# Hybrid decoder layer: gate and up's products and transposes pinned to program order on TensorE, two small norm loads moved

## The chip, the cores and the metric

The kernel runs on one core of a Trainium2 chip. A core has five engines with queues of their own: TensorE (PE, matmuls and transposes), VectorE (DVE), ScalarE (ACT), GpSimd (POOL) and SyncE (SP, which issues most DMAs here). The metric is the device time of one execution in microseconds (us); lower is better.

## The reference

A decoder layer on 1024 rows of width 1024, all in float32:

```
x = x + 0.5 * SwiGLU_1(RMSNorm(x))          # w_gate, w_up: 1024 x 2816, w_down: 2816 x 1024
h = RMSNorm(x); p = h @ W_in
o_A = dilated window attention(p)            # 8 heads of 64; q and k are normed per head
o_B = latent attention(p)                    # 4 heads
x = x + W_out [RMSNorm(o_A); RMSNorm(o_B)]
x = x + 0.5 * SwiGLU_2(RMSNorm(x))

SwiGLU(h) = (silu(h @ w_gate) * (h @ w_up)) @ w_down
```

The change touches the two SwiGLU blocks (FFN1 and FFN2 below) and the loads of the two norm weights `dil_q_norm` and `dil_k_norm` of o_A's heads.

## The kernel before, in words

**Products.** Each float32 operand is split into a high part (an ACT copy, L104) and a low part (a DVE subtraction, L105). `products()` then issues, for each of four blocks of 128 rows, three matmuls: high by high (L125), high by low (L126), low by high (L127). One product of the FFN is thus 12 matmuls of 128x512, all into one PSUM bank. There are eight banks (`ps()`).

**Gate and up by Strassen's scheme.** The 2816 columns are cut into 11 pairs c = 0 to 10. For each pair and each of gate ("g") and up ("u"), in short a unit such as 0g, seven products replace eight: M11, M12, S1, S3, S2, S4, M22. The activations' operands (B11, B21, B22, T1 to T4) are made once from the transposed, normed rows. The weights' operands (S1 to S4 are sums and differences of weight blocks, L326) are made ahead by `prepare()`; AHEAD is 5 products. For c < FRONT = 4, M11 and M12 run first, for all pairs, while the later rows still arrive, and their sum goes to DRAM (`p1`). So a unit with c < 4 later runs only:

```
middle:  S1 -> Dk,  S3 -> E,  S2 -> A;   a = kept + A (L583);  q = a + E (L584);  q = q + Dk (L585)
close:   S4 -> Dk (accumulates);  q = a + Dk (L593);  M22 -> E (accumulates);  a = a + E (L597)
```

`kept` is M11+M12 read back from `p1`. The program's order for these pairs is middle(0g), close(0g), middle(0u), close(0u), middle(1g), and so on. From c = 4 on, M11 and M12 of the next unit are written between a middle and its close; for 3u they are those of 4g.

**What sets the order.** A scheduler builds every engine's order from the program and from a modelled timeline; a bare instruction may be moved past its neighbours if its data allow it. `tc.keep_in_program_order(i)` ties an instruction to the one of the same engine that was traced before it, as an order of issue. `behind_operands()` places DVE's sums behind the low parts of the next operands (LEAD = 3).

**Start of an FFN.** `bank(th, k)` makes one bank of transposed rows: four 128x128 transposes (L232), one from each row tile. Tiles `y[0]` to `y[3]` are half 0 of the rows and `y[4]` to `y[7]` half 1, which `second_half()` turns between the early products. Row norms go ACT (squares), POOL (L193, L135, L136: the reciprocal root), DVE (scaling).

**Norm weights.** `qkgain`, two columns of 128, is loaded by two POOL DMAs (L81) at the start of the kernel, and its first column is scaled by DVE (L82). It is used in the attention part, far behind FFN1. `rel_bias_rows()` prepares the attention's bias rows; it is called beside FFN1, in pieces.

Of the kernel before, what the change touches and what calls it, by code (L numbers as in the profile page):

```python
# [13 lines left out]
ALU = mybir.AluOpType  # L14
# [4 lines left out]
P = 128  # L19
# [11 lines left out]
HD = 64  # L31
# [30 lines left out]
def tile_layer(ctx: ExitStack, tc: tile.TileContext, x, g1n, mixn, g2n, wg1, wu1, wd1, wg2, wu2, wd2,  # L62
               w_in, dqn, dkn, rel_t, qan, wqb, kvan, wkvb, mqn, mkn, ond, onm, w_out,
               cs, onehot, mask, out):
    nc = tc.nc
# [8 lines left out]
    ident = cpool.tile([P, P], F32, name="ident")  # L74
# [2 lines left out]
    nc.gpsimd.memset(neghalf, -0.5)  # L77
    qkgain = cpool.tile([P, 2], F32, name="qkgain")
    kpss = cpool.tile([P, NT], F32, name="kpss")
    for i, src in enumerate((dqn, dkn)):  # L80
        nc.gpsimd.dma_start(qkgain[:, i:i + 1], bass.AP(src.tensor, src.offset, [[0, 2], [1, HD], [1, 1]]))  # L81
    nc.vector.tensor_scalar(qkgain[:, 0:1], qkgain[:, 0:1], -HD ** -0.5, None, op0=ALU.mult)  # L82

    count = [0]

    def nm(s):
        count[0] += 1
        return f"{s}_{count[0]}"

    def slot(shape, dt=F32):  # L90
        return slots.tile(shape, dt, tag="slot", name=nm("slot"))

    def tmp(shape, dt=F32):
        return tpool.tile(shape, dt, tag="tmp", name=nm("tmp"))

    def small(w):
        return spool.tile([P, 8], F32, tag="small", name=nm("small"))[:, :w]

    def ps():
        return psum.tile([P, 512], F32, tag="ps", name=nm("ps"))  # L100
# [16 lines left out]
        split(hi[:, :cols], lo[:, :cols], raw[:, :cols])  # L117
        return hi, lo

    def products(pt, pairs, first=True):  # L120


        total = len(pairs)
        for i, ((ah, al), (bh, bl)) in enumerate(pairs):
            nc.tensor.matmul(pt, ah, bh, start=first and i == 0, stop=False, skip_group_check=not first)  # L125
            nc.tensor.matmul(pt, ah, bl, start=False, stop=False, skip_group_check=not first)  # L126
            nc.tensor.matmul(pt, al, bh, start=False, stop=i == total - 1, skip_group_check=not first)  # L127

    def cut(pair, a, b):
        return pair[0][:, a:b], pair[1][:, a:b]  # L130
# [92 lines left out]
    def ffn(rows_in, ys, gain, wg, wu, wd, act_d, xsrc, done, lead, aside=iter(())):  # L223
# [2 lines left out]

        y = {}

        def bank(th, k):
            pt = ps()  # L230
            for i in range(4):
                nc.tensor.transpose(pt[:, i * P:(i + 1) * P], y[4 * th + i][:, k * P:(k + 1) * P], ident)  # L232
            return pt

        B11, B21, B22, T1, T2, T3, T4 = (Block() for _ in range(7))
        w21, b12 = [], []

        def column(kf):
            return gcol[:, kf:kf + 1]

        def plain(of, k, pt, kf):

            if k % 2 == 0:
                of.append(slot([P, 2, 512]))
            nc.scalar.activation(of[-1][:, k % 2, :], pt, AF.Copy, scale=column(kf))

        def half(of, k):
            return of[k // 2][:, k % 2, :]

        def second_half():  # L250


            for k in range(4):
                plain(b12, k, bank(1, k), k)
            yield
            banks = [bank(1, 4 + k) for k in range(4)]
            yield
            t1 = []
            for k in range(4):
                hi, lo = B11.hi_lo(k)  # L260
                t1.append(tmp([P, 512]))
                nc.vector.tensor_tensor(t1[k], hi.bitcast(F32), lo.bitcast(F32), op=ALU.add)
                nc.vector.tensor_tensor(t1[k], half(b12, k), t1[k], op=ALU.subtract)
                T1.put(k, t1[k])
                B22.put(k, banks[k], column(4 + k))
                t = half(b12, k)
                nc.vector.scalar_tensor_tensor(t, banks[k], column(4 + k), t, op0=ALU.mult, op1=ALU.subtract)
                nc.vector.scalar_tensor_tensor(t1[k], banks[k], column(4 + k), t1[k], op0=ALU.mult, op1=ALU.subtract)
                yield
            for k in range(4):  # L270
                T3.put(k, half(b12, k))
            yield
            for k in range(4):
                T2.put(k, t1[k])
            yield
            for k in range(4):
                t = half(w21, k)
                nc.vector.tensor_tensor(t, t, t1[k], op=ALU.subtract)
                T4.put(k, t)
            yield  # L280
# [30 lines left out]
        def make(c, nme, which):  # L311
            front = c < FRONT and which in ("M11", "M12")
            u = (front, c, nme)
            load_units(units.index(u) + (3 if front else 2))
            f1, f2 = raws[u][0], raws[u][-1]
            m = {"M11": f1[:, :512], "M12": f1[:, 512:], "M21": f2[:, :512], "M22": f2[:, 512:]}
            need = {"S1": ("M21", "M22", ALU.add), "S2": ("S1", "M11", ALU.subtract),
                    "S3": ("M11", "M21", ALU.subtract), "S4": ("M12", "S2", ALU.subtract)}
            if which in need:

                a_, b_, op = need[which]
                if which == "S1":
                    sums_["S1"] = tmp([P, 512])
                s1 = sums_["S1"]
                src = {"S1": s1, "S3": m["M21"], "S2": s1, "S4": m["M12"]}[which]
                nc.vector.tensor_tensor(src, s1 if a_ == "S1" else m[a_], s1 if b_ == "S2" else m[b_], op=op)  # L326
            else:
                src = m[which]
            s = slot([P, 2, 512], F32R)
            lows.append(split(s[:, 0, :], s[:, 1, :], src))  # L330
            ready[(c, nme, which)] = (s[:, 0, :], s[:, 1, :])
            if which == "M22" or (front and which == "M12"):
                del raws[u]
# [8 lines left out]
        def prepare(n):  # L342
            while made[0] < min(used[0] + n, len(order)):
                make(*order[made[0]])
                made[0] += 1

        def product(pt, c, nme, which, blk, first=True, ahead=AHEAD):
            assert order[used[0]] == (c, nme, which)
            prepare(ahead + 1)
            used[0] += 1  # L350
            w = ready.pop((c, nme, which))
            products(pt, [(cut(w, k * P, (k + 1) * P), blk.hi_lo(k)) for k in range(4)], first)

        acts = {}

# [67 lines left out]
        for t in range(4 + lead):  # L423
            y[t] = ys(t)
        prepare(1)
        for k in range(4):
            B11.put(k, bank(0, k), column(k))
        prepare(2)
        banks = [bank(0, 4 + k) for k in range(4)]
        for k in range(4):  # L430
            B21.put(k, banks[k], column(4 + k))
        sums = second_half()

        def hook(n):
# [123 lines left out]
        def start(c, nme):  # L558

            A, Bk = ps(), ps()  # L560
            product(A, c, nme, "M11", B11)
            product(Bk, c, nme, "M12", B21)
            q = tmp([P, 512])
            nc.scalar.activation(q, A, AF.Copy)
            with behind_operands():
                nc.vector.tensor_tensor(q, q, Bk, op=ALU.add)  # L566
            return A, q
# [81 lines left out]
    def rel_bias_rows():  # L649
        oh = [slot([P, RW // 2]) for _ in range(2)]  # L650
        br = [slot([P, RW // 2]) for _ in range(2)]
        rt = small(8)
        nc.gpsimd.memset(rt[:33, :], 1.0)
        nc.sync.dma_start(rt[:32, :], rel_t)
        w = RW // 2
        for c in range(2):
            nc.sync.dma_start(oh[c][:33, :], onehot[:, c * w:(c + 1) * w])
        yield
        for c in range(2):
            for j in range(2):  # L660
                pt = ps()
                sl = slice(j * w // 2, (j + 1) * w // 2)
                nc.tensor.matmul(pt[:8, :w // 2], rt[:33, :8], oh[c][:33, sl], start=True, stop=True)
                nc.vector.tensor_copy(br[c][:8, sl], pt[:8, :w // 2])
            nc.gpsimd.dma_start(brd[:, c * w:(c + 1) * w], br[c][:8, :])
        for i in range(2):
            nc.gpsimd.dma_start(bd[:, :, i, :], bass.AP(brd.tensor, brd.offset + i * NEAR + 127,
                                                        [[RW, DH], [-1, P], [1, 256]]))
        yield

    def columns(src, col, width):
# [17 lines left out]
    def mid(t, xt):  # L689
# [11 lines left out]
        defer(2 if t < 4 else 4, turn)  # L701

    ffn(load_rows, lambda t: norm_rows(x0.pop(t), both=t < 4), g1n, wg1, wu1, wd1, act_d, x, mid, 0, rel_bias_rows())


# [643 lines left out]
    def fin(t, xt):  # L1349
        nc.sync.dma_start(out[t * P:(t + 1) * P, :], xt)  # L1350

    ffn(lambda t: None, last_rows, g2n, wg2, wu2, wd2, act_d, x2, fin, 2)
    flush()

# [75 lines left out]
```

## Time and profile before

| | us |
|---|---|
| runs: median (3) | 1892.15 |
| runs: lowest, highest | 1885.06, 1893.9 |
| profiled execution, own time | 1884.57 |
| its span | 1882.8 |
| PE busy in the span | 1821.7 (97%) |
| DVE, ACT, POOL busy | 1241.4, 789.9, 295.3 |
| FFN1, gate and up and down | 0 to about 640 |
| attention | about 640 to 1200 |
| FFN2 | about 1200 to 1880 |

The span is what the profile of one execution covers; that execution's own time is 1.8 us more. In the profile's rows an engine is busy while it executes; matmuls overlap, one of 128x512 lasts 0.39 us, but the next starts after about 0.23. Matmul rows are of a modelled end, and a few can be missing.

### The profile page before, as it was taken

The numbers are of one execution on the slowest core, as the hardware profiler recorded it, in microseconds if no ns is written. First come the engines' busy times: TensorE is split into PE (matmuls) and PEld (weight loads), VectorE is DVE, ScalarE is ACT, GpSimd is POOL, SyncE is SP. The second block draws the span as 40 slices with busy tenths as digits, with TensorE's granted clock in tenths as the row PEclk, the third lists the DMA queues.
The fourth block names the chain that finished last, engine by engine and source line by source line (L and its number), as shares of the span: only waits on it lengthen the run. The fifth ranks groups of instructions, "written<-read, shape, count | busy, mean of one in ns | idle before, by whom it ended". The sixth has DMA issues, their size and how long they took to land.

```text
span 1882.8 us, 25065 instructions
## 1 busy us (share of the span) xinstructions
PE 1821.7 (97%) x9040; PEld 1534.8 (82%) x9040; DVE 1241.4 (66%) x2375; ACT 789.9 (42%) x1802; POOL 295.3 (16%) x508
## 2 busy tenths in 40 slices
PE   7998999999999999999998999998999999999998
PEld 6776888888888888889997988886778888888887
DVE  5867767666968273327878783467776766778671
ACT  6422332334445152235876682363223333343540
POOL 3011010000000122423455520210111000100000
PEclk9999999999999999999999999999999999999999
DMA  7334233325943241023311232333433322388412
GB/s 252 123 120 145 107 133 116 116 74 201 383 148 112 95 139 34 29 57 113 96 31 36 69 118 101 117 146 106 156 101 134 107 86 94 115 306 294 124 56 90
DMA packets 92325, 234.38 MB, mean 124 GB/s; under 512 B 12486, under 2 KB 18328, under 8 KB 92200
## 3 DMA queue, kind: packets, MB, share of 16 engines
q1 hardware_dynamic: 71592, 162.93, 26.1%
q0 software_dynamic: 20608, 69.85, 10.6%
q8 instruction: 71, 1.16, 0.3%
q14 instruction: 54, 0.44, 0.1%
HBM read 165.00 MB, written 63.53 MB: 121 GB/s over the span
## 4 chain that ended last, share of the span: by engine, by line
PE 86%; DVE 8%; ACT 2%; issue 2%; DMA 1%; SPq 0%; POOL 0%; DVEq 0%; POOLq 0%; ACTq 0%
PE ps L127 19%; PE ps L125 18%; PE ps L126 18%; PE ps L516 7%; PE ps L517 7%; PE ps L515 7%; DVE slot L105 2%; PE ps L839 2%; PE ps L865 1%; PE ps L813 1%; PE ps L904 1%; PE ps L829 1%; DMA slot<-in_wg_dram 1%; ACT slot L104 1%; PE ps L1027 1%
## 5 line engine op out<-in xcount | busy, mean ns | idle before, releaser
L125 PE MATMUL ps<-slot,slot 128*128 128x512 f32 (+3 forms) x1712 | 659.1, 387 | 11.9 <-ACT slot L104 9.6
L127 PE MATMUL ps<-slot,slot 128*128 128x512 f32 (+3 forms) x1712 | 652.4, 385 | 13.8 <-DVE slot L105 13.8
L126 PE MATMUL ps<-slot,slot 128*128 128x512 f32 (+3 forms) x1712 | 655.7, 383 | 3.6 <-DVE slot L105 3.6
L127 PEld LDWEIGHTS ps<-slot,slot 128*128 128x128 f32 x1712 | 323.2, 189 | 81.2 <-DVE slot L105 19.5
L125 PEld LDWEIGHTS ps<-slot,slot 128*128 128x128 f32 x1712 | 323.0, 189 | 80.4 <-ACT slot L104 16.7
L126 PEld LDWEIGHTS ps<-slot,slot 128*128 128x128 f32 x1712 | 323.2, 189 | 65.5 <-DVE slot L105 4.4
L105 DVE TENSOR_TENSOR slot<-slot,slot 128x512 fp32r<-128x512 f32 (+1 forms) x428 | 293.2, 704 | 42.9 <-ACT slot L104 41.2
L104 ACT ACTIVATE slot<-slot 128x512 fp32r<-128x512 f32 (+1 forms) x428 | 261.0, 638 | 110.3 <-PE ps L517 49.0
L104 ACT ACTIVATE slot<-tmp 128x512 fp32r<-128x512 f32 x258 | 160.5, 626 | 311.3 <-DVE tmp L326 212.7
L516 PE MATMUL ps<-slot,slot 128*128 128x512 f32 x616 | 239.9, 390 | 0.0
L517 PE MATMUL ps<-slot,slot 128*128 128x512 f32 x616 | 239.7, 389 | 0.0
L515 PE MATMUL ps<-slot,slot 128*128 128x512 f32 x616 | 237.0, 389 | 0.0
L105 DVE TENSOR_TENSOR slot<-tmp,slot 128x512 fp32r<-128x512 f32 x258 | 176.4, 687 | 21.6 <-ACT slot L104 21.0
L515 PEld LDWEIGHTS ps<-slot,slot 128*128 128x128 f32 x616 | 115.6, 188 | 24.0
L516 PEld LDWEIGHTS ps<-slot,slot 128*128 128x128 f32 x616 | 115.6, 188 | 24.0
L517 PEld LDWEIGHTS ps<-slot,slot 128*128 128x128 f32 x616 | 115.6, 188 | 23.9
L593 DVE TENSOR_TENSOR tmp<-tmp,ps 128x512 f32<-128x512 f32 x44 | 30.3, 688 | 135.2 <-PE ps L127 135.2
L601 ACT ACTIVATE tmp<-tmp 128x512 f32<-128x512 f32 x80 | 50.3, 629 | 157.7 <-DVE tmp L593 118.1
L523 DVE SCALAR_TENSOR_TENSOR slot<-ps,slot 128x512 f32<-128x512 f32 x56 | 37.4, 688 | 81.4 <-PE ps L517 81.4
L821 ACT ACTIVATE slot<-slot,tmp 128x256 f32<-128x256 f32 (+1 forms) x128 | 59.7, 468 | 27.6 <-DVE tmp L814 26.9
L136 POOL TENSOR_TENSOR small<-small,neghalf 128x1 f32<-128x1 f32 (+2 forms) x68 | 66.6, 982 | 5.0
L566 DVE TENSOR_TENSOR tmp<-tmp,ps 128x512 f32<-128x512 f32 x28 | 19.3, 688 | 72.6 <-PE ps L127 72.6
(180 smaller groups left out, 1995.3 us busy)
## 6 DMA issues: line engine op xcount, KB each, us to landing
tmp<-act SPq DMA_DIRECT2D x154, 256.0 KB
act<-slot POOLq DMA_DIRECT2D x58, 512.0 KB, 5.0
slot<-in_wg_dram SPq DMA_DIRECT2D x52, 512.0 KB
slot<-in_wu_dram SPq DMA_DIRECT2D x52, 512.0 KB
slot<-in_wd_dram SPq DMA_DIRECT2D x40, 512.0 KB
slot<-in_x_dram SPq DMA_DIRECT2D x16, 512.0 KB
x_mid<-slot POOLq DMA_DIRECT2D x16, 512.0 KB, 3.7
slot<-x_mid SPq DMA_DIRECT2D x16, 512.0 KB
```

The costliest lines, as they stand in the source:

```text
L104: nc.scalar.activation(hi, src, AF.Copy)
L105: return nc.vector.tensor_tensor(lo, src, hi.bitcast(F32), op=ALU.subtract)
L125: nc.tensor.matmul(pt, ah, bh, start=first and i == 0, stop=False, skip_group_check=not first)
L126: nc.tensor.matmul(pt, ah, bl, start=False, stop=False, skip_group_check=not first)
L127: nc.tensor.matmul(pt, al, bh, start=False, stop=i == total - 1, skip_group_check=not first)
L136: nc.gpsimd.tensor_tensor(r, r, neghalf[:, :w], op=ALU.pow)
L515: nc.tensor.matmul(banks[i], ah, w[:, 0, :], start=first and k == 0, stop=False, skip_group_check=not first)
L516: nc.tensor.matmul(banks[i], ah, w[:, 1, :], start=False, stop=False, skip_group_check=not first)
L517: nc.tensor.matmul(banks[i], al, w[:, 0, :], start=False, stop=k == KD - 1, skip_group_check=not first)
L601: nc.scalar.activation(q, q, AF.Silu)
L821: nc.scalar.activation(self.p[:, e, :w], self.p[:, e, :w], AF.Exp, bias=self.m[e], scale=-1.0, accum_out=self.den[e])
L839: nc.tensor.matmul(po[:, e * HD:(e + 1) * HD], self.pt[:, n * P:(n + 1) * P], self.head["values"](self.far, self.j, e, j - nb + 1), start= ...
```

## The change

Three edits.

1. All matmuls of gate's and up's products are pinned by `tc.keep_in_program_order` (argument `pin` of `products()`, given by `product()`). Other users of `products()` are not pinned.
2. `bank()` becomes `turned()`: several banks are transposed together, one row tile after the other through all banks, and the transposes are pinned. Half 0's eight banks are made together before the first operands are.
3. The two loads of `qkgain` and DVE's scaling of it move into `rel_bias_rows()`, pinned.

In the changed file L125, L126, L127 are L122, L124, L126; L105 is L102; L326 is L328; L583, L584, L585 are L586, L587, L588; L593 and L597 are L596 and L600.

```
-    for i, src in enumerate((dqn, dkn)):
-        nc.gpsimd.dma_start(qkgain[:, i:i + 1], bass.AP(src.tensor, src.offset, [[0, 2], [1, HD], [1, 1]]))
-    nc.vector.tensor_scalar(qkgain[:, 0:1], qkgain[:, 0:1], -HD ** -0.5, None, op0=ALU.mult)
...
-    def products(pt, pairs, first=True):
+    def products(pt, pairs, first=True, pin=lambda i: i):
...
-            nc.tensor.matmul(pt, ah, bh, start=first and i == 0, stop=False, skip_group_check=not first)
...
+            pin(nc.tensor.matmul(pt, ah, bh, start=first and i == 0, stop=False,
+                                 skip_group_check=not first))
...
-        def bank(th, k):
-            pt = ps()
+        def turned(th, ks):
+            pts = [ps() for _ in ks]
             for i in range(4):
-                nc.tensor.transpose(pt[:, i * P:(i + 1) * P], y[4 * th + i][:, k * P:(k + 1) * P], ident)
-            return pt
+                for pt, k in zip(pts, ks):
+                    tc.keep_in_program_order(
+                        nc.tensor.transpose(pt[:, i * P:(i + 1) * P], y[4 * th + i][:, k * P:(k + 1) * P], ident))
+            return pts
...
-            for k in range(4):
-                plain(b12, k, bank(1, k), k)
+            for k, pt in enumerate(turned(1, range(4))):
+                plain(b12, k, pt, k)
             yield
-            banks = [bank(1, 4 + k) for k in range(4)]
+            banks = turned(1, range(4, 8))
...
-            products(pt, [(cut(w, k * P, (k + 1) * P), blk.hi_lo(k)) for k in range(4)], first)
+            products(pt, [(cut(w, k * P, (k + 1) * P), blk.hi_lo(k)) for k in range(4)], first,
+                     tc.keep_in_program_order)
...
+        banks = turned(0, range(8))
         for k in range(4):
-            B11.put(k, bank(0, k), column(k))
+            B11.put(k, banks.pop(0), column(k))
         prepare(2)
-        banks = [bank(0, 4 + k) for k in range(4)]
...   (in rel_bias_rows)
+        for i, src in enumerate((dqn, dkn)):
+            tc.keep_in_program_order(
+                nc.gpsimd.dma_start(qkgain[:, i:i + 1], bass.AP(src.tensor, src.offset, [[0, 2], [1, HD], [1, 1]])))
...
+        tc.keep_in_program_order(
+            nc.vector.tensor_scalar(qkgain[:, 0:1], qkgain[:, 0:1], -HD ** -0.5, None, op0=ALU.mult))
```

How the order moves, at three places. On PE, the end of S2 of unit 0g in FFN1, before (ps_155 is its bank A, ps_148 its Dk, ps_149 its E; ps_163 and ps_164 are Dk and E of the next unit, 0u; slots are operands):

```order
L125 MATMUL ps_155_762<-slot_138_665,slot_135_656 128x512
L125 MATMUL ps_163_823<-slot_109_513,slot_153_731 128x512
L126 MATMUL ps_163_823<-slot_110_514,slot_153_731 128x512
L126 MATMUL ps_155_762<-slot_139_666,slot_135_656 128x512
L127 MATMUL ps_155_762<-slot_138_665,slot_135_656 128x512
L125 MATMUL ps_164_824<-slot_129_626,slot_154_747 128x512
L126 MATMUL ps_164_824<-slot_130_627,slot_154_747 128x512
L127 MATMUL ps_163_823<-slot_109_513,slot_153_731 128x512
```

The rest of S1 and S3 of 0u, M22 of 0g and two matmuls of S2 of 0u follow; S4 of 0g (into ps_148) begins 36 matmuls behind the last of S2. And now:

```order
L122 MATMUL ps_155_759<-slot_138_662,slot_135_653 128x512
L124 MATMUL ps_155_759<-slot_139_663,slot_135_653 128x512
L126 MATMUL ps_155_759<-slot_138_662,slot_135_653 128x512
L122 MATMUL ps_148_720<-slot_111_514,slot_140_681 128x512
L124 MATMUL ps_148_720<-slot_112_515,slot_140_681 128x512
```

S4 of 0g stands directly behind S2's last matmul; M22 of 0g follows, then S1, S3, S2 of 0u, each whole.

On DVE, the sums behind S2 of unit 1g, before (ps_189 is A, ps_183 E, ps_182 Dk):

```order
L583 TENSOR_TENSOR tmp_192_994<-tmp_190_976,ps_189_975 128x512
L105 TENSOR_TENSOR slot_188_960<-slot_166_827,slot_188_960 128x512
L383 TENSOR_TENSOR slot_180_928<-slot_180_928,slot_175_886 128x512
L326 TENSOR_TENSOR tmp_186_942<-tmp_186_942,slot_165_825 128x512
L584 TENSOR_TENSOR tmp_193_995<-tmp_192_994,ps_183_937 128x512
L385 TENSOR_TENSOR slot_181_929<-slot_178_908,slot_180_928 128x512
L326 TENSOR_TENSOR slot_165_825<-slot_165_825,tmp_186_942 128x512
L585 TENSOR_TENSOR tmp_193_995<-tmp_193_995,ps_182_936 128x512
```

And now:

```order
L586 TENSOR_TENSOR tmp_192_991<-tmp_190_973,ps_189_972 128x512
L102 TENSOR_TENSOR slot_196_1016<-slot_166_824,slot_196_1016 128x512
L587 TENSOR_TENSOR tmp_193_992<-tmp_192_991,ps_183_934 128x512
L588 TENSOR_TENSOR tmp_193_992<-tmp_193_992,ps_182_933 128x512
L596 TENSOR_TENSOR tmp_195_1013<-tmp_192_991,ps_182_933 128x512
```

One low part is left between the three sums, where five operations stood before; L596, the sum behind S4, is next.

On POOL, the end of row 7's norm in FFN1, before:

```order
L193 TENSOR_TENSOR small_69_294<-small_67_290 128x1
L135 TENSOR_SCALAR small_70_296<-small_69_294 128x1
L653 MEMSET small_282_1531 33x8
L136 TENSOR_TENSOR small_70_296<-small_70_296,neghalf_77 128x1
L401 DMA p1_88<-slot_76_328 128x1024
```

And now:

```order
L193 TENSOR_TENSOR small_69_291<-small_67_287 128x1
L135 TENSOR_SCALAR small_70_293<-small_69_291 128x1
L656 MEMSET small_282_1528 33x8
L663 DMA qkgain_79<-in_dqn_dram 128x1x1
L663 DMA qkgain_79<-in_dkn_dram 128x1x1
L136 TENSOR_TENSOR small_70_293<-small_70_293,neghalf_77 128x1
L404 DMA p1_85<-slot_76_325 128x1024
```

The two loads of the norm weights stand between two steps of the last row's norm.

More of the change, by code (lines that the diff above doesn't have):

```diff
@@ L118, in load_unit @@
         return hi, lo
-    def products(pt, pairs, first=True):
+    def products(pt, pairs, first=True, pin=lambda i: i):
         total = len(pairs)
         for i, ((ah, al), (bh, bl)) in enumerate(pairs):
-            nc.tensor.matmul(pt, ah, bh, start=first and i == 0, stop=False, skip_group_check=not first)
-            nc.tensor.matmul(pt, ah, bl, start=False, stop=False, skip_group_check=not first)
-            nc.tensor.matmul(pt, al, bh, start=False, stop=i == total - 1, skip_group_check=not first)
+            pin(nc.tensor.matmul(pt, ah, bh, start=first and i == 0, stop=False,
+                                 skip_group_check=not first))
+            pin(nc.tensor.matmul(pt, ah, bl, start=False, stop=False,
+                                 skip_group_check=not first))
+            pin(nc.tensor.matmul(pt, al, bh, start=False, stop=i == total - 1,
+                                 skip_group_check=not first))
     def cut(pair, a, b):
```

## The prediction

> **What bounds the kernel now.** I read the page first (engine shares, the chain that ended last, the costliest groups), then the waits of TensorE (PE), then windows of time, then single instructions where the windows show loss.
>
> ```profile
> span 1882.8 us, 25065 instructions
> PE 1821.7 (97%) x9040; PEld 1534.8 (82%) x9040; DVE 1241.4 (66%) x2375; ACT 789.9 (42%) x1802; POOL 295.3 (16%) x508
> PE 86%; DVE 8%; ACT 2%; issue 2%; DMA 1%; SPq 0%; POOL 0%; DVEq 0%; POOLq 0%; ACTq 0%
> ...
> PE ps L127 <- DVE slot L105: 13.8, 13, 1.6
> PE ps L232 <- DVE slot L198: 11.9, 2, 11.5
> PE ps L125 <- ACT slot L104: 9.6, 13, 1.1
> ...
> PE ps L126 <- DVE slot L105: 3.6, 2, 1.8
> ```
>
> PE is the bound: busy 97% of the span and 86% of the chain. The waits (us in total, times, longest) say where it idles. The 11.9 us at L232 are the kernel's start, for the input rows. The other three lines, 27.0 us in 28 waits, are matmuls of gate and up that wait for the high part (ACT, L104) or the low part (DVE, L105) of an operand. Only these can be won back.
>
> ```profile
> 60.00:95.40 35.40, 31.02 (x127) 24.36 (x125) 28.40 (x48) 12.43 (x23) 2.71 (x5) 0.95 0.37 126
> 95.40:190.00 94.60, 84.91 (x352) 66.12 (x352) 64.24 (x106) 23.57 (x40) 12.54 (x21) 0.98 0.40 136
> 200.00:300.00 100.00, 100.00 (x443) 82.00 (x442) 67.59 (x112) 32.57 (x56) 10.82 (x15) 1.00 0.37 127
> 1275.00:1300.00 25.00, 20.55 (x82) 15.90 (x81) 19.83 (x34) 10.87 (x20) 2.46 (x5) 0.93 0.39 132
> 1300.00:1400.00 100.00, 91.56 (x385) 72.10 (x384) 69.91 (x115) 25.60 (x44) 12.52 (x21) 0.98 0.40 136
> ...
> 1400.00:1500.00 100.00, 100.00 (x443) 82.81 (x442) 67.69 (x110) 34.53 (x61) 7.97 (x12) 1.00 0.29 106
> ```
>
> Each row: window, its length, then busy time and count for PE, weight loads, DVE, ACT, POOL, then granted clock. In 200 to 300 and 1400 to 1500 PE never rests: 443 matmuls in 100 us, 0.2257 us each. By that rate the four other windows lose 35.4-127x0.2257 = 6.7, 94.6-352x0.2257 = 15.2, 25-82x0.2257 = 6.5 and 100-385x0.2257 = 13.1 us, 41.5 us together. All of it lies where the pairs c=0 to 3 run S1, S3, S2, S4, M22 (their M11 and M12 were done earlier), once in each FFN. That is all the change can win.
>
> **What pinning does there.** S4 accumulates into bank Dk, which S1 filled, and DVE must first read Dk for the sum over S2 (L583 reads S2's bank, L584 adds E, L585 adds Dk). So S4 waits for L585. Before, the scheduler put other products between.
>
> ```profile
> 77.30 0.39 PE L127 MATMUL ps<-slot,slot 128*128 128x512 f32 x1
> 78.68 0.50 PE L125 MATMUL ps<-slot,slot 128*128 128x512 f32 x1 [1.00 <-ACT slot L104]
> ...
> 81.03 0.50 PE L127 MATMUL ps<-slot,slot 128*128 128x512 f32 x1 [1.61 <-DVE slot L105]
> 81.37 0.39 PE L125 MATMUL ps<-slot,slot 128*128 128x512 f32 x1
> ...
> 90.46 0.39 PE L125 MATMUL ps<-slot,slot 128*128 128x512 f32 x1
> ...
> 92.95 0.62 PE L127 MATMUL ps<-slot,slot 128*128 128x512 f32 x2
> ...
> 95.45 0.50 PE L125 MATMUL ps<-slot,slot 128*128 128x512 f32 x1
> ...
> 1301.49 0.39 PE L125 MATMUL ps<-slot,slot 128*128 128x512 f32 x1
> ...
> 80.29 0.69 DVE L105 TENSOR_TENSOR slot<-tmp,slot 128x512 fp32r<-128x512 f32 x1
> ...
> 83.89 0.68 DVE L585 TENSOR_TENSOR tmp<-tmp,ps 128x512 f32<-128x512 f32 x1
> ...
> 93.38 0.69 DVE L593 TENSOR_TENSOR tmp<-tmp,ps 128x512 f32<-128x512 f32 x1 [7.00 <-PE ps L127]
> ...
> 193.80 0.68 DVE L584 TENSOR_TENSOR tmp<-tmp,ps 128x512 f32<-128x512 f32 x1
> 194.52 0.69 DVE L585 TENSOR_TENSOR tmp<-tmp,ps 128x512 f32<-128x512 f32 x1
> ...
> 1290.02 0.69 DVE L585 TENSOR_TENSOR tmp<-tmp,ps 128x512 f32<-128x512 f32 x1
> ```
>
> For the first gate unit S2's last matmul starts at 77.30; L585 ends at 83.89+0.68 = 84.57; S4 starts at 90.46, with 36 matmuls of the next unit and M22 in between. Afterwards S4's first matmul stands right behind S2's last.
>
> Short windows around the two first units, columns as above:
>
> ```profile
> 71.78:75.19 3.41, 1.64 (x7) 1.04 (x6) 3.41 (x7) 3.41 (x7) 1.07 (x2) 1.00 0.99 382
> ...
> 78.61:82.02 3.41, 1.72 (x6) 1.15 (x7) 3.41 (x6) 0.02 (x1) 0.54 (x1) 1.00 0.19 54
> 82.02:85.43 3.41, 3.41 (x9) 2.64 (x9) 3.41 (x7) 2.00 (x4) 0.00 (x0) 0.50 0.06 23
> ...
> 1283.52:1286.93 3.41, 0.98 (x4) 0.30 (x2) 3.41 (x6) 0.63 (x1) 0.54 (x1) 1.00 0.11 25
> 1286.93:1290.34 3.41, 3.18 (x8) 2.50 (x9) 3.41 (x7) 0.78 (x2) 0.00 (x0) 0.50 0.14 52
> ```
>
> *First unit of each FFN.* DVE fills these windows (3.41 of 3.41) and is the bound there, so L585 ends no earlier than 84.57. S4 then starts 0.05 later (the L105 at 80.29 ended at 80.98, and the matmul that waited for it started at 81.03), its first matmul takes 0.34 in place of 0.227 (81.03 to 81.37), and five products follow up to the point that before reaches at 95.45: 84.62+0.11+60x0.2267 = 98.33, so +2.9. In FFN2 the same from 1290.71: 1304.47 against 1301.49, +3.0.
>
> *The other closes with no cover.* 0u, 1g, 1u, 2g, 2u and 3g: six in each FFN. From the last matmul's start to DVE's first read 0.43 (92.95 to 93.38); L583 to L584 and L584 to L585 0.72 each, the spacing of dependent ones (193.80 to 194.52); L585 0.69; 0.05 to the matmul; 0.11 for its slow start; less 0.227 for the normal step: 2.49. In gate units from 1g on the new DVE order has one L105 between L583 and L584, about 0.5 more: 2.97. Three of each: 16.4 us for each FFN. In return these stretches' own losses go, since S4 and M22 give ACT and DVE five products of lead: 15.2 and 13.1. Net +1.2 and +3.3. The ends: 2.1 a close if the DVE steps are 0.60 apart as independent ones are, 3.6 if two more operations slip in.
>
> *Covered closes.* For 3u and all c from 4 on, M11 and M12 of the next unit stand between S2 and S4, in both kernels.
>
> ```profile
> 230.15 0.39 PE L125 MATMUL ps<-slot,slot 128*128 128x512 f32 x1
> ...
> 231.70 0.69 DVE L585 TENSOR_TENSOR tmp<-tmp,ps 128x512 f32<-128x512 f32 x1
> ...
> 235.59 0.39 PE L125 MATMUL ps<-slot,slot 128*128 128x512 f32 x1
> ```
>
> S2 ends near 230.15, L585 at 232.39, M12 near 235.59: 3.2 us to spare, so nothing. If that cover were gone, 2.5 us for each of 30 closes.
>
> **The small parts.** The norm weights' loads and their DVE scaling leave the start; PE's start waits for input rows, so 0 (at most 0.5). On POOL the two loads now stand ahead of the last step of row 7's norm (L136):
>
> ```profile
> 1.31 1.03 POOL L81 DMA_DIRECT2D qkgain<-in_dqn_dram  x1 [0.35 <-issue]
> 2.34 0.82 POOL L81 DMA_DIRECT2D qkgain<-in_dkn_dram  x1
> ...
> 32.23 0.63 POOL L136 TENSOR_TENSOR small<-small,neghalf 128x1 f32<-128x1 f32 x1
> ```
>
> That step and the four transposes that need it come 1.85 later. The queued matmuls cover some of it; between 0 and 1.85 I take 0.9, the middle, because pinned transposes hold the banks that DVE reads next. Transposing several banks row by row in FFN2 delays its first operand by up to 2 us, of which earlier products cover more than half: 0.7, between 0 and 2.
>
> Sum so far: 0.9+2.9+1.2+0.7+3.0+3.3 = +12.0.
>
> **The clock.** Bubbles have a second price, in the short windows above. The granted clock is 0.50 for 3.41 us after a window with 6 matmuls or fewer (78.61, 1283.52), and was not lowered after one with 7 (71.78). Two of the four such windows in these stages are shown, all on one grid of 3.41 us; the sums above already credit the old ones. A half-clock window issues 9 where 15 would go: 1.4 to 1.7 us, say 1.5. A window has 6 matmuls or fewer if at least 3.41-6.5x0.2267 = 1.94 us of a bubble falls in it. For a bubble of 2.49 that fails when the grid cuts it so that neither part reaches 1.94, 1.39/3.41 = 41% of positions; for 2.97, 27%. So 66% of twelve closes dip: 12x0.66x1.5 = 11.9, and the two long first bubbles for certain: 3.0.
>
> The Trainium skill ("TensorE: Matmul & The Clock Gate", Part 1 and "HAM oscillation") puts the free-running window at 3413 ns, which the trace has, and gives as its practical rule no PE gap over about 3.4 us. By that rule only the two first bubbles would dip and the sum would be +15; the row from 78.61, whose waits of 1.00 and 1.61 us were each under 3.4, dips all the same, so I go by the rows.
>
> Forecast: +27 on the profiled execution's own 1884.57, 1911.5. That execution lies 7.6 below the runs' median of 1892.15 (1885.06 to 1893.9); with half of this added I take 1915.
>
> **Rivals.** *Bubbles without dips* (the rule above, or luck with the grid): +12 to +15, 1896.5 to 1899.5 on the profiled scale, 1900 to 1903 on the median's. For it: one window that came as near as 7 matmuls did not dip. Chance 0.20.
>
> *Even exchange:* the first units start their chain earlier and the small parts are hidden, so only 12 closes at 2.1 to 2.5 against 28.3 lost: -3 to +2, 1882 to 1894. For it: 27 us of operand waits really go. Against: DVE had no gap before L585 of the first unit. 0.10.
>
> *Faster, a short close:* DVE reads E and Dk so early that only L585 follows S2. With 7.5 for the rest (0.9+2.9+0.7+3.0), 12b-28.3+7.5 is below zero for a close of b under 1.73 us and reaches -9.5 under 0.94. At 0.9 it gives 1874.6, on the median's scale 1878. Against: L584 takes L583's result, L585 takes L584's, and L583 needs S2. 0.10.
>
> *Worse:* every close dips and some of the 30 covered closes are exposed by half a microsecond: 12+3+18+15 = +48, 1933 to 1940. 0.08.
>
> The forecast itself, 1903 to 1933, has 0.52. A measurement of this kernel tells about 0.5% (9.4 us) from no change. Slower by more: 0.52+0.08+half of the no-dip case = 0.70; within: 0.10+0.08 = 0.18; faster: 0.12, the short close and the lucky edge of the exchange. The range 1890 to 1933 leaves out the short close, the worse case and a little of the exchange, about 2 in 10.
>
> **What would show it.** In the changed profile the waits of PE should list L122 (the first matmul of a product) behind DVE L588, the former L585: 14 times, about 48 us, the longest near 7.5. The waits for L101 and L102 on operands should nearly go. The clock should show 8 to 12 half-clock windows between 75 and 190 and as many between 1280 and 1400, less what the grid spares (if two only: the no-dip rival). 200 to 300 should still read 443 matmuls. Wrong I am if L588 is not what S4 waits for, if those waits are nearer 1 us, or if the first unit's L588 ends well before 84.

## The result, and the profile after

The changed kernel takes 1911.69 us (median of 4, 1909.44 to 1916.01) against 1889.52 for the kernel before, timed with it (median of 4, 1885.06 to 1893.9): a ratio of 1.012, 95% interval 1.0087 to 1.0153. The profiled execution is the slowest of the four, 1916.01 with a span of 1914.2, and is compared with the 1884.57 of before: +31.4. All executions compared below agree with the others of their kernel within 1%, except one of e9_early_alone that took 3958.96 us, for a reason that is not known.

The page (span, engine shares, chain):

```profile
span 1914.2 us, 25117 instructions
PE 1835.1 (96%) x9040; PEld 1548.7 (81%) x9040; DVE 1245.8 (65%) x2375; ACT 793.8 (41%) x1802; POOL 294.8 (15%) x508
PE 85%; DVE 9%; ACT 2%; issue 2%; DMA 2%; POOL 1%; SPq 0%; DVEq 0%; ACTq 0%; POOLq 0%
```

PE's largest wait over the whole run (us in all, times, longest), and what PE's instructions that write PSUM banks waited for in all (us, times):

```profile
PE ps L122 <- DVE tmp L588: 31.8, 12, 3.3
```

```profile
  ACT slot L101: 13.7, 2
  DVE slot L198: 7.9, 2
  DVE slot L102: 5.1, 3
```

The waits on operands (L101, L102) fell from 27.0 us in 28 to at most 18.8 in 5, and two of these five, 13.7 us, are closes too (the first of each FFN, below). In their place stand twelve waits for L588, the former L585. The wait at the start for L198 fell from 11.9 to 7.9.

The same windows as before, with 0.2257 us for a matmul:

```profile
60.00:100.00 40.00, 28.36 (x110) 22.32 (x109) 30.88 (x51) 13.96 (x25) 2.71 (x6) 0.87 0.26 86
100.00:200.00 100.00, 86.44 (x332) 69.00 (x331) 63.32 (x101) 22.42 (x37) 12.54 (x21) 0.88 0.41 133
200.00:300.00 100.00, 100.00 (x443) 81.99 (x442) 64.48 (x107) 31.62 (x54) 9.65 (x14) 1.00 0.33 108
1275.00:1300.00 25.00, 23.21 (x98) 18.80 (x97) 25.00 (x41) 14.85 (x28) 3.24 (x6) 0.95 0.49 169
1300.00:1400.00 100.00, 81.35 (x328) 64.82 (x328) 65.32 (x104) 24.19 (x40) 9.98 (x17) 0.93 0.35 113
1400.00:1500.00 100.00, 96.65 (x414) 79.51 (x414) 67.57 (x110) 32.23 (x56) 8.37 (x13) 0.97 0.33 111
```

All loss lies again where c is 0 to 3: 15.2, 25.1, 2.9, 26.0 and 6.6, together 75.8 against 41.5. The window 200 to 300 still holds 443 matmuls: the covered closes cost nothing. The granted clock, third number from the right, is 0.87 to 0.97 in the five windows that lose, against 0.93 to 0.98 before.

Both traces hold 9040 matmuls. The start of the n-th one (counted from 0) in each tells where the change stood at that point, after minus before in us:

| place | matmul | after - before |
|---|---|---|
| first transpose | 0 | -3.89 |
| first product of FFN1 | 32 | -5.05 |
| last operands before 0g's close | 288 | -4.52 |
| c = 4 nearly reached, FFN1 | 700 | +13.83 |
| end of attention | 5800 | +14.75 |
| gate and up of FFN2 begin | 6260 | +16.07 |
| c = 4 reached, FFN2 | 6920 | +31.46 |
| last matmul | 9039 | +31.46 |

So the two stages with uncovered closes (closes without other products in front of S4) cost 18.4 and 15.4 us. The start gave 5.1, of which 0.5 was lost again before the first close; attention and the way into FFN2 took 0.9 and 1.3.

The first close of FFN1, an up close and a gate close, PE's rows of the changed kernel (start, length, operation, wait and its releaser):

```profile
72.30 0.39 PE L126 MATMUL ps<-slot,slot 128*128 128x512 f32 x1
80.21 0.76 PE L122 MATMUL ps<-slot,slot 128*128 128x512 f32 x1 [7.53 <-ACT slot L101]
...
96.42 0.39 PE L126 MATMUL ps<-slot,slot 128*128 128x512 f32 x1
99.12 0.47 PE L122 MATMUL ps<-slot,slot 128*128 128x512 f32 x1 [2.32 <-DVE tmp L588]
...
114.17 0.39 PE L126 MATMUL ps<-slot,slot 128*128 128x512 f32 x1
117.36 0.77 PE L122 MATMUL ps<-slot,slot 128*128 128x512 f32 x1 [2.79 <-DVE tmp L588]
```

DVE's rows at the first two:

```profile
79.38 0.69 DVE L588 TENSOR_TENSOR tmp<-tmp,ps 128x512 f32<-128x512 f32 x1
...
96.84 0.69 DVE L586 TENSOR_TENSOR tmp<-tmp,ps 128x512 f32<-128x512 f32 x1 [4.81 <-PE ps L126]
97.56 0.69 DVE L587 TENSOR_TENSOR tmp<-tmp,ps 128x512 f32<-128x512 f32 x1
98.29 0.69 DVE L588 TENSOR_TENSOR tmp<-tmp,ps 128x512 f32<-128x512 f32 x1
```

From S2's last matmul to S4's first, less a normal step of 0.227, it is 7.69, 2.47 and 2.96 us. The first wait is put down to an ACT copy (L101); L588 ended at 80.07, 0.14 before S4 began, as in the up close, so it may as well have been L588. The up close reads as a chain: S2's last matmul starts at 96.42, L586 follows 0.42 later, L587 and L588 start 0.72 and 0.73 after the one before, L588 takes 0.69, and S4 starts 0.14 after it.

The matmuls of 0.76 and 0.77 at a stall's end run at half clock; the ones behind them take 0.63 each and start 0.43 apart. Windows of 3.41 us around the gate close (they lie 0.15 behind the clock's own steps, hence the 0.98 and 0.52):

```profile
113.43:116.85 3.42, 1.13 (x5) 0.59 (x4) 2.92 (x6) 0.64 (x2) 0.92 (x2) 0.98 0.98 316
116.85:120.26 3.41, 2.90 (x7) 2.36 (x8) 0.36 (x1) 0.63 (x1) 0.00 (x0) 0.50 0.21 78
120.26:123.67 3.41, 3.41 (x9) 2.64 (x9) 0.82 (x2) 0.09 (x1) 0.00 (x0) 0.52 0.00 0
123.67:127.08 3.41, 3.41 (x16) 2.79 (x16) 2.91 (x5) 2.13 (x4) 0.00 (x0) 1.00 0.09 12
```

One close brings two half-clock windows. The first begins inside the wait and starts 7 matmuls, and another follows it. That one is full, and the clock comes back. (A row counts every matmul that touches its window, so the 9 of the full one are 8 starts and one begun before.)

### The profile page after: what moved, and what is told of

Read it like the earlier page. It is cut to its first block, busy times and chain, and to the rows that moved or that the text cites. A ratio compares the mean times of both kernels' runs of the same rounds, so it can differ in the third digit from the quotient of the medians.

```text
span 1914.2 us, 25117 instructions
## 1 busy us (share of the span) xinstructions
PE 1835.1 (96%) x9040; PEld 1548.7 (81%) x9040; DVE 1245.8 (65%) x2375; ACT 793.8 (41%) x1802; POOL 294.8 (15%) x508
## 4 chain that ended last, share of the span: by engine, by line
PE 85%; DVE 9%; ACT 2%; issue 2%; DMA 2%; POOL 1%; SPq 0%; DVEq 0%; ACTq 0%; POOLq 0%
PE ps L122 18%; PE ps L124 18%; PE ps L126 18%; PE ps L520 7%; PE ps L519 7%; PE ps L518 7%; DVE slot L102 2%; PE ps L847 2%; PE ps L873 1%; PE ps L821 1%; PE ps L912 1%; ACT slot L101 1%; PE ps L837 1%; PE ps L1035 1%; DMA slot<-in_wu_dram 1%
## 5 line engine op out<-in xcount | busy, mean ns | idle before, releaser
L122 PE MATMUL ps<-slot,slot 128*128 128x512 f32 (+3 forms) x1712 | 668.4, 391 | 48.7 <-DVE tmp L588 31.8
L124 PE MATMUL ps<-slot,slot 128*128 128x512 f32 (+3 forms) x1712 | 662.1, 387 | 3.6 <-DVE slot L102 3.6
L126 PE MATMUL ps<-slot,slot 128*128 128x512 f32 (+3 forms) x1712 | 661.5, 387 | 0.0
L122 PEld LDWEIGHTS ps<-slot,slot 128*128 128x128 f32 x1712 | 327.1, 191 | 118.5 <-issue 36.5
L124 PEld LDWEIGHTS ps<-slot,slot 128*128 128x128 f32 x1712 | 327.8, 191 | 66.6 <-DVE slot L102 4.4
L126 PEld LDWEIGHTS ps<-slot,slot 128*128 128x128 f32 x1712 | 326.7, 191 | 63.9
L102 DVE TENSOR_TENSOR slot<-slot,slot 128x512 fp32r<-128x512 f32 (+1 forms) x428 | 294.4, 704 | 36.1 <-ACT slot L101 33.9
L101 ACT ACTIVATE slot<-slot 128x512 fp32r<-128x512 f32 (+1 forms) x428 | 260.7, 638 | 104.3 <-PE ps L520 44.8
L101 ACT ACTIVATE slot<-tmp 128x512 fp32r<-128x512 f32 x258 | 160.5, 626 | 314.1 <-DVE tmp L328 211.0
L102 DVE TENSOR_TENSOR slot<-tmp,slot 128x512 fp32r<-128x512 f32 x258 | 176.4, 687 | 21.6 <-ACT slot L101 21.3
L596 DVE TENSOR_TENSOR tmp<-tmp,ps 128x512 f32<-128x512 f32 x44 | 30.3, 688 | 80.3 <-PE ps L126 79.8
L587 DVE TENSOR_TENSOR tmp<-tmp,ps 128x512 f32<-128x512 f32 x44 | 30.2, 686 | 65.4 <-ACT tmp L583 65.2
L569 DVE TENSOR_TENSOR tmp<-tmp,ps 128x512 f32<-128x512 f32 x28 | 19.3, 688 | 81.4 <-PE ps L126 81.4
```

Source lines behind the costliest of these rows:

```text
L101: nc.scalar.activation(hi, src, AF.Copy)
L102: return nc.vector.tensor_tensor(lo, src, hi.bitcast(F32), op=ALU.subtract)
L122: pin(nc.tensor.matmul(pt, ah, bh, start=first and i == 0, stop=False, skip_group_check=not first))
L124: pin(nc.tensor.matmul(pt, ah, bl, start=False, stop=False, skip_group_check=not first))
L126: pin(nc.tensor.matmul(pt, al, bh, start=False, stop=i == total - 1, skip_group_check=not first))
```

## The experiments

Each was timed beside the kernel before. Its median there was 1887.27 in the first group (e1, e2, e4, e5), 1886.94 in the second (e3, e6, e7, e8) and 1888.02 for e9. The ratios and intervals are those on record and not quotients of two medians, from which they differ by up to 0.2%.

**e1_loads: the third edit alone.**

```
-    (two loads of qkgain by POOL and DVE's scaling, at the kernel's start)
+    (the same, in rel_bias_rows)
```

> The kernel before with the third edit alone: the two norm-weight loads and their scaling move behind the bias rows' loads. Theory: DVE no longer waits for the load until 8.53 and row 3 of the input lands about 5 us sooner (9.3 in place of 14.4), so the first transpose starts near 7.6 in place of 11.46, the first product near 14.5 in place of 19.4, and the lead of 4 to 5 us lasts to the end: 1884 to 1886 against 1889.5. Rival, my prediction's: the start waits for input rows in any case, and the time is 1889 within 1 us.

1881.91 us, ratio 0.9978 (0.9966 to 0.999). First transpose 7.53, first product 14.15, before 19.43 (PE's rows of before, then of this kernel). The lead over before is 4.8 us at the last matmul. The time lies below the 1884 to 1886 expected, but so did the kernel before in this group (1887.27 in place of 1889.5); 5.4 less by the medians is the 4 to 5 of the theory, with half a microsecond on top. The theory holds; my prediction's "0, at most 0.5" for this was wrong.

```profile
19.43 0.50 PE L125 MATMUL ps<-slot,slot 128*128 128x512 f32 x1 [0.80 <-DVE slot L218]
```

```profile
7.53 5.82 PE L229 MATMUL ps<-ident,slot 128*128 128x128 f32 x32 [7.53 <-DVE slot L195]
14.15 0.50 PE L122 MATMUL ps<-slot,slot 128*128 128x512 f32 x1 [0.80 <-DVE slot L215]
```

**e8_scale: which half of that edit.**

```
-    nc.vector.tensor_scalar(qkgain[:, 0:1], ...)      # at the start; the two loads stay there
+    (in rel_bias_rows)
```

> The kernel before with DVE's scaling of the norm weight moved, and the two loads left at the start. Two theories on the gain of e1_loads. By DVE's wait: DVE is free at the start, and the first product starts near 14.5: 1881 to 1883. By the loads' small packets: the first transposes start near 7.6, but input row 3 lands near 14 as before, so the first product starts near 19 and the time is 1886 to 1889.

1886.62 us, ratio 0.9994 (0.9974 to 1.0015): no gain is seen. PE's start in this kernel:

```profile
7.50 1.97 PE L231 MATMUL ps<-ident,slot 128*128 128x128 f32 x8 [7.50 <-DVE slot L197]
...
17.25 3.74 PE L231 MATMUL ps<-ident,slot 128*128 128x128 f32 x16 [5.52 <-DVE slot L197]
21.26 0.50 PE L124 MATMUL ps<-slot,slot 128*128 128x512 f32 x1 [0.27 <-DVE slot L217]
```

ACT's squares of row 3, which wait for its landing, in the kernel before, here, and then in e1_loads:

```profile
14.37 0.63 ACT L191 ACTIVATE slot<-slot 128x512 f32<-128x512 f32 x1 [5.43 <-DMA slot<-in_x_dram]
```

```profile
16.09 0.63 ACT L190 ACTIVATE slot<-slot 128x512 f32<-128x512 f32 x1 [6.76 <-DMA slot<-in_x_dram]
```

```profile
8.91 0.63 ACT L188 ACTIVATE slot<-slot 128x512 f32<-128x512 f32 x1 [0.58 <-DMA slot<-in_x_dram]
```

The transposes of the first rows start as early as with the whole edit, but the squares of row 3 can only start at 16.09 in place of 8.91. The loads hold the row back, not DVE's wait for them.

**e2_products: the first edit alone.**

```
+            pin(...)   # all products of gate and up; transposes and loads as before
```

> The kernel before with the products pinned and nothing else. Theory: all of the loss is in this edit: twelve closes of 2.5 and 3.0 us, one of 7.7 and one of 6.5, and the half-clock windows behind them, about +18 in FFN1 and +15 in FFN2, with no gain at the start: 1918 to 1928. Rival: the transposes and loads carry part of the loss, and this one stays under 1908.

1918.08 us, ratio 1.0176 (1.015 to 1.0203). PE's largest wait here (L589 is the former L585):

```profile
PE ps L125 <- DVE tmp L589: 31.5, 12, 3.4
```

The closes are 2.47, 2.66 to 2.96 and 3.51 us, the first ones 6.1 and 7.7, much as in the changed kernel. The whole loss is here: 30.8 us by the medians, more than the 22.2 of the three edits together. With e1_loads (-5.4) and e3_turned (+3.9, below) the single edits add up to 29.3; whether the 7 us between are an interplay or the scatter of this kernel's four runs (1913.81 to 1922.86) stays open.

**e3_turned: the second edit alone.**

```
-        def bank(th, k):            # one bank at a time, free
+        def turned(th, ks):         # several, row tile by row tile, pinned
```

> The kernel before with the second edit alone: transposes made several banks at a time and pinned. Theory: it is no part of the loss or the gain, within 2 us of before (1885 to 1890). Rival: it delays the later rows' operands and costs 3 us or more.

1890.86 us, ratio 1.002 (1.0003 to 1.0036): +3.9 by the medians, which is the rival's, but between 0.6 and 6.8 by the interval, so neither answer is ruled out. Its trace has two half-clock windows at 17.7 to 24.5, behind the start, where before has none, and one more in attention; at c = 4 of FFN1 it stands 1.0 behind before. How much of it is the edit and how much where the window's grid fell stays open.

**e4_fill: keep PE busy in the wait.**

```
             product(A, c, nme, "S2", T2, first=c < FRONT)
+            if c < FRONT and (c, nme) != (FRONT - 1, "u"):
+                idle = ps()
+                for _ in range(9):
+                    tc.keep_in_program_order(
+                        nc.tensor.matmul(idle, T2.hi_lo(0)[0][:, :P], T2.hi_lo(0)[0], start=True, stop=True))
```

> The changed kernel with nine idle matmuls (2.03 us) into a spare bank behind S2 of the 13 units before 3u of c < 4 in each FFN's gate and up (seven closes, 0g to 3g), so that PE is busy for most of the wait. Their result is not used. Theory: the waits for L588 shrink to about 0.5 and the sums stay where they are, so nothing is won on the bubbles themselves, but the clock stays at 1.00 behind the twelve short closes; that gives back 15 to 20 of the 22.6 us that the half-clock matmuls cost: 1892 to 1898. Rival: the clock costs little, the bubble all: 1908 to 1914, or more if the idle matmuls come on top.

(The units are seven in each FFN, fourteen in all.) 1898.08 us, ratio 1.0073 (1.0056 to 1.009): 13.6 us less than the changed kernel's 1911.69, with 126 matmuls more. The two were not timed side by side; each against its own kernel before is +22.2 and +10.8, which leaves 11.4, and by the two ratios it is 9. What is left of the short closes is 0.44 (up), 0.92 (gate) and 1.47 (3g), so S4 starts as late as in the changed kernel. One stretch of FFN2 in the changed kernel and here:

```profile
1310.00:1395.00 85.00, 72.47 (x298) 58.11 (x297) 53.57 (x84) 20.27 (x33) 8.47 (x15) 0.95 0.36 118
```

```profile
1310.00:1395.00 85.00, 82.67 (x361) 66.97 (x360) 57.02 (x92) 18.92 (x33) 11.04 (x19) 1.00 0.41 134
```

The clock is 1.00 behind all short closes; only the two long first ones still lower it, for two windows each. The half clock behind the short closes was thus some 9 to 14 us of the change's loss. The theory expected 15 to 20, reckoned from the 22.6 us of the changed kernel's profiled execution, its slowest; the time came out at the edge of its 1892 to 1898.

**e7_fill3: three in place of nine.**

```
-                for _ in range(9):
+                for _ in range(3):
```

> As e4_fill with three idle matmuls in place of nine, so that of each short close 1.8 us (up units) or 2.3 us (gate units) of idle PE are left. Theory of the window (half clock after a window of 3.41 us with at least 1.94 us of idle PE): no half-clock window behind the six up closes, one behind about half of the six gate closes; 1896 to 1906. Rival: any wait of more than a microsecond lowers the clock as often as in the changed kernel, 17 half-clock windows in the two stages; 1908 to 1914.

1905.49 us, ratio 1.0099 (1.0069 to 1.0129). An up close, then a gate close (L585 are the idle matmuls, L593 the sum):

```profile
97.99 0.47 PE L122 MATMUL ps<-slot,slot 128*128 128x512 f32 x1 [1.64 <-DVE tmp L593]
98.30 0.40 PE L124 MATMUL ps<-slot,slot 128*128 128x512 f32 x1
...
114.64 0.63 PE L122 MATMUL ps<-slot,slot 128*128 128x512 f32 x1 [2.11 <-DVE tmp L593]
115.06 0.63 PE L124 MATMUL ps<-slot,slot 128*128 128x512 f32 x1
```

After waits of 1.80 (up), none of six is followed by half-clock matmuls; after waits of 2.28 and 2.83 (gate), four of six. The window theory stands: it is not the wait's length alone but how much of it falls in one window. In the changed kernel 8 of the 12 short closes (2.47 to 3.51) lower the clock, and 8 of 12 in e2_products too, the 66% of the prediction. The Trainium skill ("TensorE: Matmul & The Clock Gate", Part 1, "HAM oscillation") names idle gaps over about 3.4 us as what to avoid; here 2.28 was enough in three of four cases, and the measurement decides.

**e5_early: no wait behind S2.**

```
+                q = tmp([P, 512])                      # c < FRONT, behind S3, beside S2
+                nc.scalar.activation(q, Dk, AF.Copy)
+                with behind_operands():
+                    nc.vector.tensor_tensor(q, q, E, op=ALU.add)
             product(A, c, nme, "S2", T2, first=c < FRONT)
...
                     nc.vector.tensor_tensor(a, kept, A, op=ALU.add)
-                nc.vector.tensor_tensor(q, a, E, op=ALU.add)
-                nc.vector.tensor_tensor(q, q, Dk, op=ALU.add)
+                    nc.vector.tensor_tensor(q, q, a, op=ALU.add)
```

> The changed kernel, products pinned as they are, but for c < 4 the sum is formed in another order: an ACT copy of Dk and a DVE addition of E run while S2 runs, and after S2 only A's part is added. S4 then waits for no sum behind S2. Theory: the twelve short bubbles (33 us) go with their half-clock windows (18 us or so), the first unit keeps 3 to 6 us in each FFN because operands are late there: 1848 to 1868. Rival: S4's wait isn't what costs, or DVE, with as many sums as before and an ACT copy ahead of them, becomes late for the operands: 1890 to 1915.

1846.28 us, ratio 0.98 (0.9783 to 0.9817), under the low end. These are all of PE's waits that are left from 60 to 200, FFN1's stage:

```profile
PE ps L124 <- DVE slot L102: 1.8, 1, 1.8
PE ps L122 <- DVE tmp L583: 1.2, 1, 1.2
```

Not only the short closes' waits are gone but also the first unit's, 7.53 in the changed kernel, but for 1.2 (L583 is the early sum): with the sum begun beside S2, Dk is free when S4 comes. One half-clock window is left in the two stages, at 1259.39, behind a late operand (L102) of FFN2's first unit. That S4's wait for the sum, with the half clock that it brings, is the cost is shown.

**e6_early_free: the same, nothing pinned.**

```
-            products(pt, ..., first, tc.keep_in_program_order)
+            products(pt, ..., first)
-                    tc.keep_in_program_order(nc.tensor.transpose(...))
+                    nc.tensor.transpose(...)
```

> As e5_early, with its early sums and moved loads, but neither products nor transposes pinned. Theory: pinning is worth something once the close has no wait, since a free order mixes the next unit's products in and stalls on their operands, as before: most of the 16.6 and 15.1 us of such stalls come back and the time is 1858 to 1885. Rival: the early sums alone are the gain, and pinned or free is the same: 1844 to 1850.

1845.34 us, ratio 0.9772 (0.9744 to 0.98). My theory falls, the rival holds: pinned or free is the same. The operand stalls of before didn't come from a free order as such. DVE's waits for S4 from 60 to 200, before and here (L601 is the sum behind S4, L593 in before):

```profile
DVE tmp L593 <- PE ps L127: 37.3, 7, 7.0
```

```profile
DVE tmp L601 <- PE ps L126: 2.3, 2, 2.0
```

I read this as follows. Before, S4 was pushed 36 matmuls back to get around its wait; L593, which needs S4, then held DVE's queue for 37.3 us, and the low parts behind it came late for PE. Without the wait the scheduler has no reason to push S4 back. What is shown is that the early sums take away S4's wait and the operand stalls together. That the held queue made the low parts late is argued only: in the changed kernel the sums behind S4 and S2 hold DVE for 28.4 and 15.2 us from 60 to 200 with hardly a late operand, while PE stands still as well.

**e9_early_alone: the early sums on the kernel before.** The diff is e5's, applied to the kernel before.

> The kernel before with the early sums alone: nothing pinned, transposes and loads as they were. Theory: S4's wait for the sum behind S2, and the order that the scheduler made to get around it, were the whole 36 us that gate and up lost in before; this edit wins them alone, and the loads' 5 us stay apart: 1848 to 1854. Rival: the lead of the moved loads or the joint transposes is needed for it: over 1858.

1848.46 us, ratio 0.979 (0.9769 to 0.9811); the median still holds the execution of 3958.96, and that of the other three is 1847.81. One reordering of three sums wins some 40 us with none of the three edits, and the rival falls. e6_early_free, which has the moved loads and the joint transposes beside it, is 2.5 us lower (1.4 if each is taken against its own kernel before), where the loads alone gave 5.4; why not more is left open.

## Why the prediction was right or wrong

The forecast was 1915, within 1890 to 1933; 1911.69 was measured, and the mechanism it named, S4 standing bare behind S2 and waiting for the sum, is the one that acts (e2_products, e5_early). The sum's terms did not all hold. That the time came within 4 us of the forecast is in part luck: two errors cancelled.

*The short closes:* 2.49 and 2.97 were forecast; the trace has 2.47 to 2.48 for the up closes and 2.95 to 2.96 for the gate closes, but 3.51 for 3g in both FFNs. The sum is 33.7 with those two (forecast 32.8). The rows of dependent DVE steps carried this.

*The first units:* the waits are 7.69 in FFN1 and 6.52 in FFN2, where the longest was forecast near 7.5. "L585 ends no earlier than 84.57" failed: L588 ended at 80.07. The prediction had named an end well before 84 as a sign of being wrong. It came, but not for a shorter wait: with the input earlier, S2's last matmul started 5.0 us earlier too (72.30 in place of 77.30), so the wait itself stayed.

*The return of the operand waits:* right in size, 27 us of them before, 5 after without the two closes. But the ground given, five products of lead by pinning, isn't the whole of it: in e6_early_free they are gone without pinning.

*"PE's start waits for input rows, so 0 (at most 0.5)":* wrong, -5.05. I read the row's landing as given. It was itself held up by the two loads that the change moves (e8_scale).

*The transposes and POOL:* 0.9 was forecast in FFN1, and the lead shrinks by 0.5, from 5.05 to 4.52; 0.7 was forecast before FFN2's gate and up, a middle for which the prediction shows no row, and 1.3 is there. Attention's 0.9, with one more half-clock window, was not in the sum.

*The clock:* the share (66%) held, and the condition (1.94 us of idle PE in one window) held within 0.15: in the gate and up stages of all traces, counting 0.227 us of work for each matmul that starts, no window with under 1.95 us of idle PE was followed by half clock, and every one with over 2.1 was; in between both occur. The size didn't hold. The sum had one window for each lowered close, ten in all (the list of signs spoke of 8 to 12 in each stage, which doesn't fit that sum). The profiled execution has 17, ten in FFN1 and seven in FFN2: 16 behind its ten lowered closes, and one behind a late operand at 1296.64. A half-clock window that began 0.66 us or more before the wait's end was followed by another, in five closes; in three closes it began at most 0.45 before that end, and none followed. The 110 or so matmuls that start some 0.43 apart in place of 0.227 make 22.6 us, forecast 14.9. This error of +7.7 and the missed gain of 5 nearly cancel. By e4_fill the short closes' clock is worth 9 to 14.

*The profiled execution against the median:* +27 was forecast on the profile's scale, +31.4 is there; in the medians it is +22.2. Where the window's grid falls against the waits differs from run to run, and the profiled one of the changed kernel was its slowest, that of before its fastest. Adding half of the 7.6 between profile and median was a guess that fitted.

*The rivals:* the short close and the even exchange are out by the measured 2.5 and 3.0. Bubbles without dips is out by the traces; e4_fill comes near to what it would have been, 1898. The worse case is out too: the covered closes cost nothing (443 matmuls in 200 to 300), and four of the twelve short closes did not dip.

## What to carry to other kernels

Before pinning an order on the busiest engine, look for what the free order was avoiding: here a product that accumulates into a bank another engine must read first. Take that wait away, by reading the early banks while the last product still runs, and the order no longer matters; pinned without that, in this kernel, twelve waits stood bare, and eight of them lowered the clock as well. And when a start waits for a transfer, look at what else those DMA engines carry before calling the landing time given.

## What was not expected of the hardware

Two loads of 0.5 KB, 4 bytes for each of 128 partitions, hold up loads of 512 KB. Windows from 5 to 10 us, before and e1_loads (the last columns are clock, DMA share, GB/s):

```profile
5.00:10.00 5.00, 0.00 (x0) 0.00 (x0) 1.37 (x5) 1.65 (x6) 0.50 (x1) 1.00 1.04 269
```

```profile
5.00:10.00 5.00, 2.47 (x12) 2.47 (x13) 3.85 (x12) 2.45 (x8) 3.73 (x9) 1.00 1.00 387
```

The DMA engines are full in both, but with the small loads they move 269 GB/s in place of 387. In that window POOL's queue, which carries the two loads, took 19.6% of the 16 engines. The trace has 32 packets of 256 bytes there, 15.4 us in all. Most took 0.08 us; four took longer, and two of these, begun at 7.75 and 7.95, took 5.55 and 5.37 us, until 13.3. The squares of row 3 begin at 14.37. In e8_scale the last long one runs from 9.76 to 15.37, and row 3's squares begin at 16.09. So it reads as if row 3 had to wait for the DMA engines that these two packets held. The trace doesn't name a packet's engine, so that is not shown, nor why a few packets take so long; with the loads moved behind the start, one of e1_loads still takes 5.08 us, at 29.93.

The half clock can feed itself: at 0.43 us a matmul a window has room for 8, so a small remainder of the wait is enough for a second half-clock window. In the rows at 116.85 and 120.26 it was 0.66 us of wait, from the clock's step at 116.70 to S4 at 117.36; 0.45 us, behind the step at 154.25, was not enough. Half-clock windows with 8 starts were never followed by another in these stages.
